# The two float32r parts of a unit of weights, interleaved column by column in one tile

## The chip, the cores and the metric

The kernel runs on one core of one Trainium2 chip. The metric is the device time of one execution, in microseconds (us). The kernel before was run twice: 1192.42 and 1192.73 us, median 1192.58 us. TensorE (PE in the rows) multiplies a stationary operand of up to 128 columns, which a weight load (PEld) puts into the array, with a moving operand of up to 512 columns; it writes to PSUM. VectorE (DVE), ScalarE (ACT) and GpSimd (POOL) work beside it, and SyncE (SP) issues most DMAs.

## The reference

A decoder trunk of two layers over 512 tokens with 1024 channels, all in float32. Layer 0 mixes tokens with an mLSTM (4 heads, projections for q, k, v, o and gates, output projection). Layer 1 mixes them with a convolution module (1024 to 2 x 1024 projection with a gate, depthwise convolution over 31 tokens, layer norm, output projection). After each mixer comes a gated MLP: a projection up to 2 x 2816 channels, a depthwise convolution over 3 tokens, `silu(a) * b`, a projection down to 1024. There is an RMS norm ahead of every mixer and MLP and one at the end:

```
x = x + mixer_i(rmsnorm(x, norm_mix[i]))
hdn = causal_dwconv(rmsnorm(x, norm_ffn[i]) @ w_up, conv_w, conv_b)
x = x + (silu(hdn[..., :D_FF]) * hdn[..., D_FF:]) @ w_down
```

## The kernel before

Activations lie with channels on partitions and tokens along the free axis: `xt[m]` is a block of 128 channels by 512 tokens. TensorE takes float32r operands, and full precision comes from splitting each operand into two float32r parts, a rounded copy (hi) and the rest (lo). A product of two float32 blocks is then three products, hi x hi, hi x lo and lo x hi, which `mm3` issues one after the other (L161 to L163); each has its own weight load.

**Weights** come in 193 units of at most 128 x 1024 float32, in the order of the list `seq`. `feed_to` issues the DMA of a unit on SyncE's queue (tile `wr`, four buffers, up to four units ahead of the one in use). It then splits the unit two units ahead (in two places one): ScalarE writes the hi part with a copy (L149) and VectorE the lo part with a subtraction (L150). The two parts are two tiles, `wh` and `wl`, from the pool `wsp` with three buffers each, and each is contiguous: column c of a part is 4 bytes after column c - 1. `next_unit` hands the pair to the stage that uses it.

**Who reads the parts.** Units 0 to 3 and 5 to 8 are the v weights; in `v_pair` they are the moving operand (512 columns at a time) and the activations are stationary. Unit 4 holds the gate weights, stationary in slices of 36 columns that start 144 bytes apart. In the 184 units from the ninth on (q, k, o, output projection, up and down projections, the convolution module's projections) slices of 128 columns of `wh` and `wl` are the stationary operand, and the activations move: `xh`/`xl` in `proj`, `gh`/`gl_` and `zh`/`zl` in `out_proj` (L576, L577, L580), `yh`/`yl` in the down projection of `ffn`. The last block of the last down projection runs in two halves of 256 tokens, so its three units are used with moving operands of 256 columns.

**What orders the work.** The program is written in one order, and a planner with its own cost estimates orders each engine's queue; semaphores between writers, readers and the release of buffers follow from the tiles. A buffer of `wsp` can be written again when the products that read it are done. In the convolution module VectorE also computes taps of the depthwise convolution (L744, `dve_tap`), handed out between the projections' products. A 128 x 128 constant, `p128`, is set by GpSimd at the start of that module, cast by ScalarE to `pdvr`, and used for one mean; it lies in the module's pool `cp`. The pool `work` has four buffers with the tag `tmp` for short-lived tiles.

Of the kernel before, what the change touches and what calls it, by code (L numbers as in the profile page):

```python
# [9 lines left out]
F32 = mybir.dt.float32  # L10
F32R = mybir.dt.float32r
# [3 lines left out]
P = 128  # L15
# [9 lines left out]
EPS = 1e-6  # L25
QSCALE = 128.0 ** -0.5
NEG = -1.0e30
NPH = 4                    # token phases of the convolution on the tensor engine
NTAU = T // NPH
NJ = (CK + 2 * NPH - 3) // NPH  # L30
GR = 68                    # rows: input gates at 0, running maximum at 32, forget gates at 64

# column offsets in the packed per-channel parameter array
_COLS = {}
_off = 0
for _n, _w in [("norm_mix", 16), ("norm_ffn", 16), ("norm_final", 8), ("mconv_w", 32),
# [9 lines left out]
def hybrid_trunk(ctx, tc, x_in, par_in, tph_in, wg_in, wv_in, wqk_in, wo_in, mout_in, cin_in,  # L46
# [6 lines left out]
    wsp = ctx.enter_context(tc.tile_pool(name="wsp", bufs=3))  # L53
    work = ctx.enter_context(tc.tile_pool(name="work", bufs=1))
# [12 lines left out]
    def small():  # L67
        return psms.tile([P, T], F32, tag="ms", name=nm("ms"))

# [1 line left out]
    par = const.tile([P, NPAR], F32, name="par")  # L71
    nc.scalar.dma_start(out=par[:, :16], in_=par_in[:, :16])

# [18 lines left out]
    G.memset(mhalf, -0.5)  # L92

    def warm(n, after=None):
        """Products that nobody reads, to keep the clock of the tensor engine up over a wait."""
        ps = bank()
        for _ in range(n):
            with tc.issue_after(after.ins) if after is not None else nullcontext():
                after = PE.matmul(ps[:, :P], ones, ones, start=True, stop=True)  # L99

# [1 line left out]
    seq = []  # L102
    for h in range(2):
        for u in range(4):
# [3 lines left out]
    for what in "q0 o0 o1 q1 o2 o3 q2 o4 q3 o5 o6 o7".split():  # L108
        i = int(what[1])
# [22 lines left out]
    st = {"dma": 0, "split": 0, "get": 0}  # L132
    raws, splits = {}, {}

    def feed_to(ndma, nsplit):
        while st["dma"] < min(ndma, len(seq)):
            i = st["dma"]
            ap, n = seq[i]
            r = wraw.tile([P, 1024], F32, tag="wr", name=f"wr{i}")
            nc.sync.dma_start(out=r[:, :n], in_=ap)  # L140
            raws[i] = r
            st["dma"] += 1
        while st["split"] < min(nsplit, len(seq)):
            i = st["split"]
            n = seq[i][1]
            r = raws.pop(i)
            hi = wsp.tile([P, 1024], F32R, tag="wh", name=f"wh{i}")
            lo = wsp.tile([P, 1024], F32R, tag="wl", name=f"wl{i}")
            st["last"] = A.copy(hi[:, :n], r[:, :n])  # L149
            V.tensor_tensor(out=lo[:, :n], in0=r[:, :n], in1=hi[:, :n], op=ALU.subtract)  # L150
            splits[i] = (hi, lo)
            st["split"] += 1
# [9 lines left out]
        PE.matmul(ps, lh, rl, start=False, stop=False)  # L162
        PE.matmul(ps, ll, rh, start=False, stop=stop)  # L163

# [1 line left out]
    xh = [None] * KD  # L166
    xl = [None] * KD

# [27 lines left out]
        return t[:, c].rearrange("p (a b) -> p a b", b=P)  # L196

    def to_rows(src, c, tag):
        """Values along the free axis, equal on all partitions -> [128 tokens, blocks]."""
        nb = (c.stop - c.start) // P  # L200
        dg = work.tile([P, T], F32, tag="tmp", name=nm("dg"), bufs=4)
        V.tensor_tensor(out=blocks(dg, c), in0=src,
                        in1=ident[:].unsqueeze(1).to_broadcast([P, nb, P]), op=ALU.mult)
        r4 = work.tile([P, NTB], F32, tag=tag, name=nm(tag))
        V.tensor_reduce(out=r4[:, :nb], in_=blocks(dg, c), op=ALU.add, axis=mybir.AxisListType.X)
        return r4

    def from_rows(r4, nb, pb):
        """[128 tokens, blocks] -> the values along the free axis on all partitions (PSUM)."""
        hl = work.tile([P, 2, NTB], F32R, tag="hl", name=nm("hl"))  # L210
        V.tensor_copy(hl[:, 0, :nb], r4[:, :nb])
        V.tensor_tensor(out=hl[:, 1, :nb], in0=r4[:, :nb], in1=hl[:, 0, :nb], op=ALU.subtract)
        for i in range(2):
            dg = work.tile([P, NTB, P], F32R, tag="tmp", name=nm("dgr"), bufs=4)
            v = V.tensor_tensor(out=dg[:, :nb], in0=ident[:].unsqueeze(1).to_broadcast([P, nb, P]),
                            in1=hl[:, i, :nb].bitcast(F32).unsqueeze(2).to_broadcast([P, nb, P]),
                            op=ALU.mult)
            p = PE.matmul(pb, onesr, dg[:, :nb].rearrange("p a b -> p (a b)"), start=i == 0, stop=i == 1)  # L218
        return v, p

    def col_mean(ps, t, c, w):
        """Sum over the partitions of t times the constant in w, on all partitions."""
        h = work.tile([P, T], F32R, tag="tmp", name=nm("ch"), bufs=4)
        l = work.tile([P, T], F32R, tag="tmp", name=nm("cl"), bufs=4)
        A.copy(h[:, c], t[:, c])
        V.tensor_tensor(out=l[:, c], in0=t[:, c], in1=h[:, c], op=ALU.subtract)
        PE.matmul(ps, w, h[:, c], start=True, stop=False)
        PE.matmul(ps, w, l[:, c], start=False, stop=True)
# [4 lines left out]
        return o4  # L233

    def row_sums(ps, t, c, w, start, stop):
        """Adds the sums over the partitions of t, times w, to ps: [128 tokens, 2 * blocks]."""
        nb = (c.stop - c.start) // P
        for b in range(nb):
            s = slice(c.start + b * P, c.start + (b + 1) * P)
            PE.matmul(ps[:, 2 * b : 2 * b + 2], t[:, s], w[:, :2], start=start and b == 0,  # L240
                      stop=stop and b == nb - 1)

    def norm_rows(nrm, c):
        """1 / rms of the tokens in c, [128 tokens, blocks]."""
        n = c.stop - c.start
        ps = small()
        col_mean(ps[:, :n], nrm.acc, c, invdr)
        r4 = to_rows(ps[:, :n].rearrange("p (a b) -> p a b", b=P), c, "ms4")
        V.tensor_scalar(out=r4[:, : n // P], in0=r4[:, : n // P], scalar1=EPS, scalar2=None,
                        op0=ALU.add)  # L250
        return rsqrt4(r4, n // P, "rs4")

    # the row factors of a norm are worked out between the first products of the next stage
    hooks = []

    def run_hook():
# [15 lines left out]

    rs = {}

    # ================= layer 0: mLSTM =================
    warm(9)
    nrm = Norm()
    first = wraw.tile([P, 1024], F32, tag="wr", name="wr0")
    for c in range(2):
        cs = slice(c * T, c * T + T)  # L280
        nc.sync.dma_start(out=first[:, cs], in_=seq[0][0][:, cs])
        nc.sync.dma_start(out=xt[c], in_=x_in[c])
    hi = wsp.tile([P, 1024], F32R, tag="wh", name="wh0")
    lo = wsp.tile([P, 1024], F32R, tag="wl", name="wl0")
    for c in range(2):
        cs = slice(c * T, c * T + T)
        A.copy(hi[:, cs], first[:, cs])
# [67 lines left out]

    pv = v_pair(0)

    # gates, channel-major: input gates on partitions 0-3, forget gates on 32-35
    wgh, wgl = next_unit()
    pg = small()  # L360
    for k in range(KD):
# [77 lines left out]
    T0 = [0, 128, 256, 256]  # L439

    def att_decay(h):
        """exp of the decay from s to t less the running maximum; s on partitions, t free."""
        plf, pm = small(), small()
        for p, i in ((plf, h), (pm, NH + h)):
            PE.matmul(p, sel[:, i, :], sth, start=True, stop=False)
# [143 lines left out]
    out_proj(gh, gl_, None, lambda m: ("norm_ffn", m))  # L589
    mctx.close()  # L590

    # ================= gated MLP with a depthwise convolution =================
    def ffn(l, g=None, last=False):
        fctx = ExitStack()
        fp = fctx.enter_context(tc.tile_pool(name=nm("ffn"), bufs=1))
# [94 lines left out]

    ffn(0, lambda m: ("norm_mix", 8 + m))

    # ================= layer 1: convolution module =================
    cctx = ExitStack()
    cp = cctx.enter_context(tc.tile_pool(name="conv", bufs=1))
    DVE_CH, POOL_CH, PE_CH = (0, 2, 4), (1,), (3, 5, 6, 7)
    NV, NG, NG4, NPRE = 5, 4, 9, 1
    cacc2 = cp.tile([P, T], F32, name="caccp")
    p128 = cp.tile([P, P], F32, name="p128")
    G.memset(p128, 1.0 / P)  # L700
    pdvr = cp.tile([P, P], F32R, name="pdvr")
    A.copy(pdvr, p128)
    cacc = {c: cp.tile([P, T], F32, name=f"cacc{c}") for c in range(8)}
    # 1 where the partition lies in the block of NPH partitions
    tph = cp.tile([P, 8 * 4 * NJ * NPH], F32, name="tph")
    nc.sync.dma_start(out=tph, in_=tph_in)
    msk4 = cp.tile([P, P // NPH, 1], F32, name="msk4")
# [74 lines left out]
                o = 32 * (2 * hf + g)  # L782
                (nc.scalar if g == 0 else nc.sync).dma_start(out=back[o : o + 32], in_=co[:, g])

    # taps for the vector engine and GpSimd, handed out between the products
    vtaps, gtaps = [], []

    def background(nv, ng):
# [9 lines left out]
    FIRST, LAST = PE_CH[0], PE_CH[-1]  # L798

    def shift():  # L800
        """The mean of one block of channels, by which all values are shifted before their sums."""
        d[FIRST] = cp.tile([P, T], F32, name=f"d{FIRST}")
        A.activation(d[FIRST].rearrange("p (t q) -> p t q", q=NPH),
                     cacc[FIRST].rearrange("p (q t) -> p t q", q=NPH), AF.Identity,
# [56 lines left out]
    sq4 = stats(4, V)  # L861
    sq7 = stats(LAST, None)

    # layer norm over channels
    pr1, pr2, pmu = small(), small(), bank()
    for i, (t1, t2) in enumerate(((s1, s2), (d[LAST], sq7))):
        row_sums(pr1, t1, slice(0, T), invd, i == 0, i == 1)
# [34 lines left out]
def _layout(inputs):  # L902
    f = {k: np.asarray(v) for k, v in inputs.items()}

    def ch(a):  # [..., C] -> [128, ... * C/128], channel c = m * 128 + p
        a = a.reshape(a.shape[:-1] + (-1, P))
        return np.moveaxis(a, -1, 0).reshape(P, -1)

    def taps(w):  # [K, C] -> [128, C/128 * K]
        k, c = w.shape  # L910
        return w.reshape(k, c // P, P).transpose(2, 1, 0).reshape(P, -1)

    def cols(w, n=P):  # [K, N] -> [N/n, 128, K/128 * n]
        k, c = w.shape
        return w.reshape(k // P, P, c // n, n).transpose(2, 1, 0, 3).reshape(c // n, P, -1)

    # gate biases: input gates on partitions 0-3, forget gates on 32-35
    bg = np.zeros((P, 1), np.float32)
    bg[0:4, 0], bg[32:36, 0] = f["m_b_gates"][0][:4], f["m_b_gates"][0][4:]
    # taps by token phase: dph[c * NPH + p, m, g, j, q] = w[K - 1 - (NPH * j + q - p), m * 128 + g * 32 + c]  # L920
    dw = f["c_dw_w"][0].reshape(CK, KD, 4, P // 4)
    dph = np.zeros((P // NPH, NPH, KD, 4, NJ, NPH), np.float32)
    for p in range(NPH):
# [50 lines left out]
```

## Time and profile before

| | |
|---|---|
| median of two runs | 1192.58 us (1192.42 to 1192.73) |
| profiled execution, first to last instruction | 1191.0 us |
| runs' median over that span | 1.6 us |
| TensorE matmul busy | 1134.3 us, 95% |
| weight loads busy | 939.7 us, 79% |
| VectorE busy | 788.6 us, 66% |
| ScalarE busy | 510.8 us, 43% |
| mean granted TensorE clock | 0.974 |

The share of busy matmul time is an upper view, since matmuls overlap in the records: one of 512 columns is recorded with about 390 ns although the next starts some 230 ns after it. So the start-to-start time, called the pitch below, is read from the records in order of time, and not from their durations.

### The profile page before, as it was taken

To read this page: it belongs to the slowest core of one execution; us is meant where nothing else is said; L and a number is where in the kernel's file an instruction comes from. 1 tells how busy PE (TensorE), PEld (TensorE's weight loads), DVE (VectorE), ACT (ScalarE), POOL (GpSimd) and SP (SyncE) were. 2 spreads that over 40 slices of the span, in tenths; PEclk is the share of its full clock that TensorE was granted. 3 is DMA by queue.
4 is the path that set the end of the run, shared out by engine and by line. 5 is a ranking of instruction groups with operands and counts; after the bars stand their busy time and mean duration, and the time that the engine had idled before them with its cause. 6 is when DMAs were issued, how large, how long until landed. Compare 5 with 4: busy or idle time off the path is not lost.

```text
span 1191.0 us, 13476 instructions
## 1 busy us (share of the span) xinstructions
PE 1134.3 (95%) x5226; PEld 939.7 (79%) x5226; DVE 788.6 (66%) x1022; ACT 510.8 (43%) x713; POOL 174.8 (15%) x126
## 2 busy tenths in 40 slices
PE   9999999999999999999998757699999999999996
PEld 7788888888888888888887647588888888888886
DVE  6788875487777775332479999874877777752222
ACT  6556774354444443222244522363544444432221
POOL 4000001100000000000267857021000000000002
PEclk9999999999999999999998879699999999999998
DMA  6222123223232323233332112022232323233322
GB/s 247 89 89 71 54 74 103 90 89 106 89 106 89 105 86 92 90 97 98 110 105 62 62 44 67 14 88 89 92 103 90 106 89 106 84 98 89 93 62 71
DMA packets 36369, 106.85 MB, mean 90 GB/s; under 512 B 4049, under 2 KB 10321, under 8 KB 36305
## 3 DMA queue, kind: packets, MB, share of 16 engines
q1 hardware_dynamic: 31728, 103.25, 27.2%
q10 hardware_dynamic: 4576, 2.74, 0.8%
q8 instruction: 41, 0.67, 0.2%
q14 instruction: 24, 0.19, 0.0%
HBM read 101.78 MB, written 2.10 MB: 87 GB/s over the span
## 4 chain that ended last, share of the span: by engine, by line
PE 84%; DVE 13%; issue 1%; ACT 1%; DMA 1%; POOL 0%; ACTq 0%; POOLq 0%; SPq 0%; DVEq 0%
PE mm L161 25%; PE mm L162 25%; PE mm L163 25%; DVE cacc L744 8%; PE mm L580 2%; PE mm L577 2%; PE mm L576 2%; DVE wl L150 2%; PE ms L240 1%; PE mm L99 0%; DMA xall<-in_dram 0%; PE ms L218 0%; DVE u L722 0%; DVE se L453 0%; DVE s L826 0%
## 5 line engine op out<-in xcount | busy, mean ns | idle before, releaser
L163 PE MATMUL mm<-xh,wl 128*128 128x512 f32 x960 | 375.6, 391 | 3.3 <-DVE wl L150 3.3
L161 PE MATMUL mm<-xh,wh 128*128 128x512 f32 x960 | 375.6, 392 | 0.0
L162 PE MATMUL mm<-xl,wh 128*128 128x512 f32 x960 | 375.4, 391 | 0.0
L150 DVE TENSOR_TENSOR wl<-wr,wh 128x1024 fp32r<-128x1024 f32 (+1 forms) x192 | 236.5, 1235 | 165.5 <-ACT wh L149 163.3
L149 ACT CAST wh<-wr 128x1024 fp32r<-128x1024 f32 (+1 forms) x192 | 197.4, 1030 | 296.1 <-PE mm L162 243.6
L163 PEld LDWEIGHTS mm<-xh,wl 128*128 128x128 f32 x960 | 181.4, 189 | 41.9 <-DVE wl L150 3.7
L162 PEld LDWEIGHTS mm<-xl,wh 128*128 128x128 f32 x960 | 181.4, 189 | 37.9
L161 PEld LDWEIGHTS mm<-xh,wh 128*128 128x128 f32 x960 | 181.5, 189 | 37.2
L193 POOL TENSOR_TENSOR acc<-acc,sq 128x512 f32<-128x512 f32 x30 | 43.3, 1444 | 746.7 <-ACT sq L191 746.2
L161 PE MATMUL mm<-yh,wh 128*128 128x512 f32 (+1 forms) x374 | 142.3, 380 | 0.0
L162 PE MATMUL mm<-yl,wh 128*128 128x512 f32 (+1 forms) x374 | 142.3, 380 | 0.0
L163 PE MATMUL mm<-yh,wl 128*128 128x512 f32 (+1 forms) x374 | 142.2, 380 | 0.0
L606 DVE TENSOR_TENSOR mm<-mm,rsb 128x512 f32<-128x512 f32 x88 | 60.8, 695 | 76.0 <-PE mm L163 73.1
L744 DVE SCALAR_TENSOR_TENSOR cacc<-u,par,cacc 128x501 f32<-128x501 f32 (+27 forms) x80 | 102.1, 1321 | 0.1
L161 PEld LDWEIGHTS mm<-yh,wh 128*128 128x128 f32 x374 | 70.0, 187 | 15.5
L162 PEld LDWEIGHTS mm<-yl,wh 128*128 128x128 f32 x374 | 70.0, 187 | 15.3
L163 PEld LDWEIGHTS mm<-yh,wl 128*128 128x128 f32 x374 | 70.0, 187 | 15.2
L616 ACT CAST yh<-ta 128x512 fp32r<-128x512 f32 x44 | 27.3, 620 | 104.6 <-DVE ta L615 104.6
L611 DVE SCALAR_TENSOR_TENSOR ta<-mm,par,ta 128x511 f32<-128x511 f32 x88 | 65.6, 745 | 1.3
L611 DVE SCALAR_TENSOR_TENSOR tb<-mm,par,tb 128x511 f32<-128x511 f32 x88 | 65.5, 746 | 1.4
L614 ACT ACTIVATE ta<-ta 128x512 f32<-128x512 f32 x44 | 27.8, 632 | 79.4 <-DVE ta L611 79.4
L741 POOL TENSOR_TENSOR cacc<-cacc,cprod 128x511 f32<-128x511 f32 (+29 forms) x30 | 49.5, 1651 | 24.1 <-ACT cprod L739 22.4
(237 smaller groups left out, 1200.5 us busy)
## 6 DMA issues: line engine op xcount, KB each, us to landing
wr<-in_dram SPq DMA_DIRECT2D x175, 512.0 KB, 3.5
wr<-in_dram SPq DMA_DIRECT2D x16, 384.0 KB, 3.1
xall<-in_dram SPq DMA_DIRECT2D x8, 256.0 KB, 6.4
us<-u ACTq DMA_DIRECT2D x16, 64.0 KB, 2.1
out_dram<-xall SPq DMA_DIRECT2D x2, 384.0 KB, 3.5
tph<-in_dram SPq DMA_DIRECT2D x1, 576.0 KB, 4.5
wr<-in_dram SPq DMA_DIRECT2D x2, 256.0 KB, 3.9
cacc<-co ACTq DMA_DIRECT2D x8, 64.0 KB, 2.4
```

What stands on the lines that cost most here:

```text
L149: st["last"] = A.copy(hi[:, :n], r[:, :n])
L150: V.tensor_tensor(out=lo[:, :n], in0=r[:, :n], in1=hi[:, :n], op=ALU.subtract)
L161: PE.matmul(ps, lh, rh, start=start, stop=False)
L162: PE.matmul(ps, lh, rl, start=False, stop=False)
L163: PE.matmul(ps, ll, rh, start=False, stop=stop)
L193: e.tensor_tensor(out=nrm.acc[:, c], in0=nrm.acc[:, c], in1=sq[:, c], op=ALU.add)
L606: V.tensor_tensor(out=ps, in0=ps, in1=rs["b"], op=ALU.mult)
L611: V.scalar_tensor_tensor(out=t[:, s:], in0=ps[:, : T - s], scalar=pcol("fconv_w", m * 3 + 2 - s), in1=t[:, s:], op0=ALU.mult, op1=ALU.add)
L614: A.activation(ta, ta, AF.Silu)
L616: A.copy(yh[:, j, :], ta)
L741: G.tensor_tensor(out=a[:, s:], in0=a[:, s:], in1=p[:, s:], op=ALU.add)
L744: V.scalar_tensor_tensor(out=cacc[j][:, s:], in0=u[:, : T - s], scalar=dw(j, CK - 1 - s), in1=cacc[j][:, s:], op0=ALU.mult, op1=ALU.add)
```

## The change

The two parts of a unit become two views of one tile of 2112 columns, from one tag with three buffers. For units 0 to 8 the views are two contiguous halves. From unit 9 on the tile is read as pairs: hi is every even column and lo every odd one, so a part's columns lie 8 bytes apart, and the pair starts at 4 x (unit number mod 16) columns, which is a multiple of 16 bytes from 0 to 240. The instructions that write and read the parts are the same in kind, number and size; only their addresses and strides differ. The pool `wsp` grows by 3 x 64 columns, 768 bytes per partition, and what is allocated behind it moves by as much. `p128` moves from the module's pool to a `tmp` buffer. Comments are removed.

```
+    def split_tile(i):
+        t = wsp.tile([P, 2048 + 64], F32R, tag="wi", name=f"wi{i}")
+        if i < 9:
+            return t[:, :1024], t[:, 1024:2048]
+        o = 4 * (i % 16)
+        v = t[:, o : o + 2048].rearrange("p (c b) -> p b c", b=2)
+        return v[:, 0], v[:, 1]
...
-            hi = wsp.tile([P, 1024], F32R, tag="wh", name=f"wh{i}")
-            lo = wsp.tile([P, 1024], F32R, tag="wl", name=f"wl{i}")
+            hi, lo = split_tile(i)
             st["last"] = A.copy(hi[:, :n], r[:, :n])
             V.tensor_tensor(out=lo[:, :n], in0=r[:, :n], in1=hi[:, :n], op=ALU.subtract)
...
-    p128 = cp.tile([P, P], F32, name="p128")
+    p128 = work.tile([P, P], F32, tag="tmp", name="p128", bufs=4)
```

## Rows read from the trace of the kernel before

**Rows 1.** The page's busy times: engine, us, share of the span, instructions.
```profile
PE 1134.3 (95%) x5226; PEld 939.7 (79%) x5226; DVE 788.6 (66%) x1022; ACT 510.8 (43%) x713; POOL 174.8 (15%) x126
```

**Rows 2.** The page's chain that ended last, shares of the span by engine.
```profile
PE 84%; DVE 13%; issue 1%; ACT 1%; DMA 1%; POOL 0%; ACTq 0%; POOLq 0%; SPq 0%; DVEq 0%
```

**Rows 3.** Busy time by window: us, PE, PEld, DVE, ACT, POOL, clock, DMA.
```profile
300.00:400.00 100.00, 100.00 (x442) 82.78 (x442) 73.62 (x93) 43.50 (x55) 0.00 (x0) 1.00 0.31 99
500.00:550.00 50.00, 50.00 (x216) 40.09 (x215) 14.13 (x15) 13.57 (x16) 3.85 (x3) 1.00 0.33 97
600.00:757.00 157.00, 113.33 (x609) 97.31 (x607) 149.25 (x138) 58.85 (x86) 102.05 (x59) 0.87 0.21 64
1163.00:1180.00 17.00, 17.00 (x149) 16.91 (x147) 3.34 (x9) 3.50 (x6) 2.18 (x3) 1.00 0.00 1
```

**Rows 4.** Groups by line and form on PE: count, busy us, mean ns, idle before.
```profile
L161 PE MATMUL mm<-xh,wh 128*128 128x512 f32 x960 | 375.6, 392 | 0.0
...
L161 PE MATMUL mm<-yh,wh 128*128 128x512 f32 x330 | 130.0, 394 | 0.0
...
L576 PE MATMUL mm<-gh,wh 128*128 128x512 f32 x48 | 18.9, 394 | 0.0
...
L161 PE MATMUL mm<-yh,wh 128*128 128x256 f32 x44 | 12.3, 279 | 0.0
```

**Rows 5.** PE in order of time, an up projection: start us, duration us, instruction.
```profile
300.28 0.39 PE L161 MATMUL mm<-xh,wh 128*128 128x512 f32 x1
...
306.40 0.39 PE L161 MATMUL mm<-xh,wh 128*128 128x512 f32 x1
```

**Rows 6.** PE in order of time, the last down projection with 512 columns.
```profile
1156.67 0.39 PE L162 MATMUL mm<-yl,wh 128*128 128x512 f32 x1
...
1163.20 0.39 PE L163 MATMUL mm<-yh,wl 128*128 128x512 f32 x1
```

**Rows 7.** PE in order of time, the last block, 256 columns.
```profile
1163.43 0.28 PE L161 MATMUL mm<-yh,wh 128*128 128x256 f32 x1
...
1172.17 0.28 PE L163 MATMUL mm<-yh,wl 128*128 128x256 f32 x1
```

**Rows 8.** PE in order of time, the output projection of layer 0.
```profile
188.32 0.39 PE L576 MATMUL mm<-gh,wh 128*128 128x512 f32 x1
...
193.89 0.40 PE L576 MATMUL mm<-gh,wh 128*128 128x512 f32 x1
```

**Rows 9.** PE in order of time, the gates: 36 stationary columns, 512 moving.
```profile
34.80 0.39 PE L161 MATMUL ms<-xh,wh 128*36 128x512 f32 x1
...
40.36 0.40 PE L163 MATMUL ms<-xh,wl 128*36 128x512 f32 x1
```

**Rows 10.** Groups by line and form of the weight loads.
```profile
L161 PEld LDWEIGHTS mm<-xh,wh 128*128 128x128 f32 x960 | 181.5, 189 | 37.2
...
L161 PEld LDWEIGHTS ms<-xh,wh 128*36 128x36 f32 x8 | 0.9, 111 | 0.8
```

**Rows 11.** Groups by line and form on DVE: the split; a strided and a plain write.
```profile
L150 DVE TENSOR_TENSOR wl<-wr,wh 128x1024 fp32r<-128x1024 f32 x14 | 21.7, 1548 | 3.0 <-ACT wh L149 2.9
...
L722 DVE SCALAR_TENSOR_TENSOR u<-mm,par,sg 128x512 f32<-128x512 f32 x4 | 4.5, 1129 | 0.0
...
L727 DVE SCALAR_TENSOR_TENSOR u<-mm,par,sg 128x512 f32<-128x512 f32 x4 | 2.9, 740 | 0.0
```

**Rows 12.** Groups by line and form on ACT: split; strided read; plain.
```profile
L149 ACT CAST wh<-wr 128x1024 fp32r<-128x1024 f32 x175 | 183.6, 1052 | 250.5 <-PE mm L162 198.0 <-issue 38.8 <-PE mm L163 11.4
...
L803 ACT ACTIVATE d<-cacc,par 128x512 f32<-128x512 f32 x1 | 1.2, 1189 | 1.2 <-DMA cacc<-co 1.2
...
L735 ACT ACTIVATE cacc<-u,par 128x512 f32<-128x512 f32 x4 | 3.1, 808 | 0.0
```

**Rows 13.** Who waited for whom: us in total, times, longest us.
```profile
ACT wh L149 <- PE mm L162: 243.6, 137, 6.2
...
PE mm L163 <- DVE wl L150: 3.3, 1, 3.3
```

More of the change, by code (lines that the diff above doesn't have):

```diff
@@ L282, in hybrid_trunk @@
         nc.sync.dma_start(out=xt[c], in_=x_in[c])
-    hi = wsp.tile([P, 1024], F32R, tag="wh", name="wh0")
-    lo = wsp.tile([P, 1024], F32R, tag="wl", name="wl0")
+    hi, lo = split_tile(0)
     for c in range(2):
```

## The prediction

> **What bounds the kernel now.** I read the busy times first, then the chain that ended last, then the windows, and last the matmuls in order of time. TensorE is busy 95% of the span, and the chain runs through it for 84% and through VectorE for 13% [rows 1, 2]. The windows say where: in an up projection (300 to 400 us) and a down projection (500 to 550) TensorE has no idle time, while VectorE is busy 73.6 of 100 us and 14.1 of 50; in the convolution module (600 to 757) it is the other way round, VectorE 149 of 157 us and TensorE 113 [rows 3]. So outside the convolution module the time is the number of products times their pitch, the time from one start to the next.
>
> The pitch is what the reader should take from the rows, at a granted clock of 1.00 throughout (2.4 GHz). In the up projection 27 steps take 6.12 us, 226.7 ns each [rows 5]; in the down projection 28 steps take 6.53 us, 233.2 ns [rows 6]; in the output projection of layer 0, 24 steps take 5.57 us, 232.1 ns [rows 8]; with 256 columns, 77 steps take 8.74 us, 113.5 ns [rows 7]. 512 columns at 2.4 GHz are 213.3 ns and 256 are 106.7, so about 13, 20, 19 and 7 ns of each step are something else. Stages with the same columns and the same loads differ by 6.5 ns, and what they differ in is which tiles are read. Every 1 ns of pitch is worth 4.25 us: the products with strided weights are 3 x 960 with `xh`, 3 x 330 with `yh`, and 2 x 192 in the two output projections, of which the 48 of L576 in layer 0 are shown [rows 4], 4254 in all, and 3 x 44 with 256 columns.
>
> **The change, part by part.** Nothing is added or removed in number; five things move.
>
> *The weight loads read 128 columns 8 bytes apart instead of 4.* No load in the trace is strided, so the price is bounded. A load of 128 columns is recorded with 189 ns, one of 36 with 111 [rows 10]: 78 ns for 92 columns, 0.85 ns each, so about 109 ns of columns and 80 ns of something fixed. With 256 columns a load is done in every 113.5 ns [rows 7], so the fixed part is overlapped and a load takes no more than that of the path. At a pitch of 226.7 ns it could become twice as long before it sets the pitch. Lower end: nothing. Upper end: twice as long, 2 x 109 = 218 ns, which with the 13 ns that a 512-column step has over its columns makes 231 ns (if those 13 ns come on top; none if they don't). I take nothing. The moving operand is the nearest row for the rate: 512 columns of 4 bytes in 226.7 ns are 9.0 bytes per ns in each partition, and a load that sweeps 1024 bytes in 109 ns needs 9.4, about what a read here already does.
>
> *The start of each slice relative to the moving tile changes from unit to unit.* The gates are the nearest row: there the same moving tiles `xh`, `xl` meet slices that start 144 bytes apart, and 24 steps take 5.56 us, 231.7 ns [rows 9], although their loads are the shortest of all. So a short load does not give a short pitch, and something in the addresses or in the 36 columns costs 5 ns against [rows 5]. Lower end, if the offsets give every stage the pitch of the up projection: 990 x 6.5 + 192 x 5.4 ns (layer 0's output projection; I leave layer 1's as it is) = -7.5 us. Upper end, if they take it from the up and `proj` products: 2880 x 5.0 = +14.4 us, or 2880 x 6.5 = +18.7 us with the pitch of [rows 6]. Within one unit all slices keep one phase, so some units should stay where they are; I take +2 us.
>
> [...]
>
> *VectorE writes the lo part with a stride.* The nearest strided write is L722, 512 bytes from element to element: 1129 ns for 512 against 740 ns for the plain form L727 [rows 11], 0.76 ns per element more. For a split of 1024 columns that would be +0.78 us, the upper end; the lower end is nothing. In the up projection VectorE would rise from 73.6 to 73.6 + 18 x 0.78 = 88 of 100 us (18 splits to 100 us, since a unit's 24 steps take 5.44 us), still hidden. Where the cover is gone, in the convolution module, 14 splits lie in VectorE's way [rows 11], 10.9 us at the upper end. I take 0, because 8 bytes are nearer to 4 than to 512. ScalarE's copy has the same bounds: the one strided read there, L803, takes 1189 ns against 808 for L735 [rows 12], 0.74 ns per element, so at most +0.76 us a unit; ScalarE is busy 43.5 of 100 us in the up projection and waits for TensorE before most copies [rows 3, 13], so both ends are hidden and cost 0.
>
> [...]
>
> *One tile has one release.* If the halves of a tile are not told apart, the hi copy of a later unit waits for the last product of the old one instead of the last but one (0.23 us), or in the output projections for eight products more (8 x 232 ns = 1.9 us), and the first product of a unit waits for the lo part, two products earlier than now (0.45 us). ScalarE waits 137 times for that release [rows 13], but as a buffer's ordinary turn: a unit is split two units, 10.9 us, ahead, so the 1.9 us are hidden; behind the waiting copy stand ScalarE's activations for the next block, which have the unit's slack too. TensorE waited for the lo part once, 3.3 us [rows 13]; that wait starts 0.45 us earlier and ends when it did. With the cover gone the price is 0.45 us for each of some 14 units in the convolution module, where the products are not the bound. I take +0.5 us.
>
> *`p128` in a `tmp` buffer:* a memset on GpSimd and a cast of 128 columns once, each under the 0.8 us of the 512 columns of L735 [rows 12]; GpSimd has room there, a `tmp` buffer must be free first and returns after the cast. No SyncE or GpSimd DMA moves. Taken: 0; upper end 1 us.
>
> **Sum.** 0 + 2 + 0 + 0 + 0.5 + 0 = +2.5 us on the profiled execution, whose span is 1191.0 us; the runs' median is 1192.6, 1.6 us above it, so 1195 us.
>
> **The rivals.**
>
> *The phase is lost everywhere in `proj` (1209 us).* The offsets bring all 2880 products to 231.7 to 233.2 ns: +14.4 to +18.7 us, mean 16.5. For it: [rows 9]. Against: those rows have 36 columns as well. Within 2%.
>
> *Strided writes stop VectorE in the convolution module (1204 us).* +10.9 us as above. Within 2%.
>
> *The loads become the bound (1248 us), the other side of the forecast.* Place: every step. If a strided load takes twice as long and its fixed overlap does not hide, a 256-column step goes from 113.5 to about 227 ns, 132 x 113.5 = +15 us, and a 512-column step to twice the load plus the 20 ns of the down projection, 238 ns: 2880 x 11.3 + 990 x 4.8 + 384 x 6 = 32.5 + 4.8 + 2.3 = +40 us; 1192.6 + 55 = 1248. It decides from a load of some 1.95 times on, where 213 ns meet the columns. For it: loads and matmuls alternate one to one and no row shows a stride. Against: the rate above. Shorter of that, the 256-column steps alone give 1208 us.
>
> *The interleave frees the moving reads (1156 us).* If part of the 13 to 20 ns is the load's reads meeting the moving reads, and a load that sweeps at the same rate as the moving operand meets them less, the excess may fall to the 7 ns of [rows 7], a pitch of 220: 2880 x 6.7 + 990 x 13.2 + 384 x 12 = 19.3 + 13.1 + 4.6 = -37 us. For it: the excess depends on tiles. Against: the gates' short loads have no smaller excess.
>
> **How the numbers follow.** No visible change (1187 to 1200): 0.41. Phase lost: 0.22. Strided writes: 0.07. Loads bound: 0.17, of which 0.07 lies between 1217 and 1232. Freed reads: 0.13, of which 0.03 lies above 1165. The forecast is the likeliest, 1195 us. The range holds the first three and what is nearest of the others, 1165 to 1232 us; 0.1 is left out on each side. Its own case alone would be 1187 to 1200. A measurement of this kernel can tell about 2%, 24 us, from no change: faster 0.13, same 0.70, slower 0.17.
>
> **What would show it.** In the profile after: weight loads with `wi` at 189 ns and the pitch in the up and down projections at 226.7 and 233.2 ns would bear out the first two steps; loads near 300 ns, or 256-column steps above 115 ns, would show the bound rival; a pitch of 220 the freed reads. L150 at its old mean would clear VectorE, at 0.78 us more convict it. A granted clock below 1.00 in the projections, or VectorE at the head of TensorE's waits there, would make the sum wrong in a way that none of these cases has.

## The result, and the profile after

The changed kernel takes 1208.97 us (median of two runs, 1208.11 to 1209.84) against 1192.58 us: the ratio is 1.0137, 95% interval [1.0108, 1.0167]. It is slower, by less than the 2% that the chances were split at and by far more than the runs scatter. The time lies in the predicted range (1165 to 1232 us), but not in the case that the forecast was made for (1187 to 1200 us, 1195 us): it is that of the rival "the phase is lost everywhere in `proj`" (1209 us).

The page after: the span and the busy times, which have the shape of [rows 1].

```profile
span 1206.4 us, 13466 instructions
...
PE 1147.5 (95%) x5226; PEld 969.6 (80%) x5226; DVE 784.8 (65%) x1022; ACT 516.6 (43%) x713; POOL 181.7 (15%) x126
```

The windows that answer to [rows 3], an up projection, a down projection and the convolution module: TensorE is still without idle time in the first two at a granted clock of 1.00, but starts 433 products in 100 us where it started 442.

```profile
300.00:400.00 100.00, 100.00 (x433) 83.89 (x432) 70.40 (x91) 43.54 (x54) 0.00 (x0) 1.00 0.30 95
500.00:550.00 50.00, 50.00 (x217) 41.95 (x216) 16.61 (x18) 14.86 (x18) 5.66 (x4) 1.00 0.34 96
600.00:757.00 157.00, 121.53 (x647) 105.35 (x645) 145.90 (x131) 60.28 (x84) 110.12 (x61) 0.89 0.22 66
```

TensorE in order of time after (start, duration): first the first and last product of 40 units of the up projection, 959 steps apart, where [rows 5] had 226.7 ns a step; then the block with 256 columns, 76 steps.

```profile
246.82 0.40 PE L170 MATMUL mm<-xh,wi 128*128 128x512 f32 x1
...
469.63 0.39 PE L172 MATMUL mm<-xh,wi 128*128 128x512 f32 x1
...
1178.03 0.28 PE L170 MATMUL mm<-yh,wi 128*128 128x256 f32 x1
...
1187.17 0.28 PE L171 MATMUL mm<-yl,wi 128*128 128x256 f32 x1
```

That is 222.81 us / 959 = 232.3 ns, and 9.14 us / 76 = 120.3 ns against 113.5 [rows 7]. Summing the time from each product's start to the next one's, by the tile that moves, over both traces:

| moving tile, columns | products | before, us | after, us | mean step without waits, before to after |
|---|---|---|---|---|
| xh, xl (512) | 2880 | 685.9 | 701.2 | 226.8 to 232.3 ns |
| yh, yl (512) | 990 | 231.0 | 230.1 | 233.3 to 232.4 ns |
| zht, zlt (512) | 192 | 44.2 | 44.9 | 229.2 to 231.8 ns |
| gh, gl (512) | 192 | 44.9 | 44.7 | 232.4 to 232.0 ns |
| yh, yl (256) | 132 | 15.3 | 16.1 | 114.2 to 120.3 ns |
| all products | 5226 | 1182.6 | 1198.0 | |

(The last column leaves out the steps that contain a wait and those at a granted clock of 0.50.) The steps of all products, waits included, make up the span but for its two ends, so both grew by 15.4 us; what the table adds is where: 15.3 of it lies at the products with `xh` and `xl`. By stage, the two up projections took 11.7 us more; none of their 2112 steps holds a wait, and 2112 x 5.5 ns is 11.6. The q and o projections of layer 0 took 3.1 us more, 384 x 5.5 ns = 2.1 by the pitch and the rest in waits. The convolution module's projections took 0.5 us more instead of 2.1: their seven steps with a wait or a change of the clock grew from 28.7 to 29.9 us, but 8 whole steps instead of 21 lay in stretches with a granted clock of 0.50, where one takes 426.7 ns, and that is some 2.6 us less.

Such a stretch of the kernel before, its window and 13 products in order of time, the first and the last:

```profile
649.20:654.30 5.10, 5.10 (x13) 3.96 (x12) 5.10 (x5) 0.81 (x3) 3.66 (x3) 0.50 0.36 103
...
649.26 0.63 PE L161 MATMUL mm<-xh,wh 128*128 128x512 f32 x1
...
654.38 0.42 PE L161 MATMUL mm<-xh,wh 128*128 128x512 f32 x1
```

5.12 us / 12 = 426.7 ns at a clock of 0.50. Half of it, 213.3 ns, is the estimate for 512 columns at a clock of 1.00, 2.4 columns a ns.

The groups that answer to [rows 10, 11, 12], and the waits of [rows 13]:

```profile
L170 PEld LDWEIGHTS mm<-xh,wi 128*128 128x128 f32 x960 | 187.7, 196 | 36.1 <-DVE se L477 0.6
...
L159 DVE TENSOR_TENSOR wi<-wr,wi 128x1024 fp32r<-128x1024 f32 x175 | 222.6, 1273 | 182.3 <-ACT wi L158 182.1
L158 ACT CAST wi<-wr 128x1024 fp32r<-128x1024 f32 x175 | 196.4, 1125 | 283.0 <-PE mm L172 222.1 <-issue 58.9 <-ACT gt L379 1.0
...
PE mm L172 <- DVE wi L159: 1.6, 2, 1.2
```

The line of all 175 splits of 1024 columns on VectorE before, which [rows 11] show for the convolution module alone:

```profile
L150 DVE TENSOR_TENSOR wl<-wr,wh 128x1024 fp32r<-128x1024 f32 x175 | 220.7, 1264 | 165.5 <-ACT wh L149 163.3
```

A load went from 189 to 196 ns, ScalarE's split from 1052 to 1125, VectorE's from 1264 to 1273. ScalarE waits for L172 now, the last product of the old unit, and not for L162; TensorE's own wait for the lo part did not grow. So the loss is, but for some 1 us in the q and o projections and as much in the convolution module, not a wait and not a busy engine: in the stages with `xh` the step from one product to the next is 5.5 ns longer.

### The profile page after: what moved, and what is told of

Same layout as the page of the kernel before. It is cut to its first block, busy times and chain, and to the rows that moved or that the text cites. A ratio compares the mean times of both kernels' runs of the same rounds, so it can differ in the third digit from the quotient of the medians.

```text
span 1206.4 us, 13466 instructions
## 1 busy us (share of the span) xinstructions
PE 1147.5 (95%) x5226; PEld 969.6 (80%) x5226; DVE 784.8 (65%) x1022; ACT 516.6 (43%) x713; POOL 181.7 (15%) x126
## 4 chain that ended last, share of the span: by engine, by line
PE 82%; DVE 13%; issue 2%; ACT 1%; DMA 1%; POOL 0%; ACTq 0%; POOLq 0%; SPq 0%; DVEq 0%
PE mm L170 25%; PE mm L171 25%; PE mm L172 25%; DVE cacc L752 7%; PE mm L588 2%; PE mm L584 2%; PE mm L585 2%; DVE wi L159 2%; PE ms L249 1%; DVE se L461 1%; PE mm L99 0%; DVE u L730 0%; DMA xall<-in_dram 0%; DVE s L834 0%; DMA us<-u 0%
## 5 line engine op out<-in xcount | busy, mean ns | idle before, releaser
L172 PE MATMUL mm<-xh,wi 128*128 128x512 f32 x960 | 378.8, 395 | 1.6 <-DVE wi L159 1.6
L170 PE MATMUL mm<-xh,wi 128*128 128x512 f32 x960 | 379.2, 395 | 0.3 <-DVE se L477 0.3
L171 PE MATMUL mm<-xl,wi 128*128 128x512 f32 x960 | 378.7, 395 | 0.0
L159 DVE TENSOR_TENSOR wi<-wr,wi 128x1024 fp32r<-128x1024 f32 (+1 forms) x192 | 238.4, 1243 | 186.1 <-ACT wi L158 186.0
L158 ACT CAST wi<-wr 128x1024 fp32r<-128x1024 f32 (+1 forms) x192 | 211.1, 1102 | 327.4 <-PE mm L172 266.5
L172 PEld LDWEIGHTS mm<-xh,wi 128*128 128x128 f32 x960 | 187.6, 195 | 38.6 <-DVE wi L159 2.5
L170 PEld LDWEIGHTS mm<-xh,wi 128*128 128x128 f32 x960 | 187.7, 196 | 36.1 <-DVE se L477 0.6
L171 PEld LDWEIGHTS mm<-xl,wi 128*128 128x128 f32 x960 | 187.5, 195 | 35.6
L170 PE MATMUL mm<-yh,wi 128*128 128x512 f32 (+1 forms) x374 | 142.7, 382 | 0.0
L171 PE MATMUL mm<-yl,wi 128*128 128x512 f32 (+1 forms) x374 | 142.7, 381 | 0.0
L172 PE MATMUL mm<-yh,wi 128*128 128x512 f32 (+1 forms) x374 | 142.6, 381 | 0.0
L172 PEld LDWEIGHTS mm<-yh,wi 128*128 128x128 f32 x374 | 72.9, 195 | 12.4
L170 PEld LDWEIGHTS mm<-yh,wi 128*128 128x128 f32 x374 | 72.9, 195 | 12.4
L171 PEld LDWEIGHTS mm<-yl,wi 128*128 128x128 f32 x374 | 72.9, 195 | 12.4
```

The lines of the kernel that those rows point to most:

```text
L170: PE.matmul(ps, lh, rh, start=start, stop=False)
```

## The experiments

The first four runs part the change into its pieces. Theory 1: the pitch is set by the start address of the stationary slice against that of the moving tile. Theory 2: by the 8-byte stride. Theory 3: by the common tile and its waits. Addresses below are those that the program assigns: tiles `wh`, `wl`, `wi`, `xh` and `xl` start 64 bytes past a multiple of 256, `yh` and `yl` at a multiple, `zht` and `zlt` 128 past one. Slices of 128 columns are 512 bytes apart (1024 with the stride), so within a unit they all keep one difference.

**e1_no_rotation**, the stride alone.

```
-        o = 4 * (i % 16)
-        v = t[:, o : o + 2048].rearrange("p (c b) -> p b c", b=2)
+        v = t[:, :2048].rearrange("p (c b) -> p b c", b=2)
```

> The changed kernel with the pair of parts always at column 0 of its tile: the parts are still 8 bytes apart, only the rotation is gone. Theory 1 (the start address of the stationary slice against the moving tile sets the pitch): the phase is constant again as before the change, so the products with xh and xl go back to 226.8 ns and those with yh to 233.3; about 1193 us. Theory 2 (the 8-byte stride of the weight load sets the pitch, whatever its start): 232.3 ns stays; about 1208 us. Theory 3 (waits from the common tile): about 1208 us with the pitch at 226.8 and idle time instead.

Measured: 1211.83 us, ratio 1.0155 [1.014, 1.0171]. The products in order of time, an up projection, 27 steps:

```profile
346.69 0.39 PE L170 MATMUL mm<-xl,wi 128*128 128x512 f32 x1
...
352.99 0.39 PE L170 MATMUL mm<-xl,wi 128*128 128x512 f32 x1
```

6.30 us / 27 = 233.3 ns, and the same in every unit. The constant start did not bring 226.8 ns back: theory 1 as it stood is wrong, and theory 2's number is off too (233.3, not 232.3). The stride by itself costs 6.5 ns a step, and the rotation takes a little of that back.

**e2_no_stride**, the rotation alone.

```
-        if i < 9:
-            return t[:, :1024], t[:, 1024:2048]
-        o = 4 * (i % 16)
-        v = t[:, o : o + 2048].rearrange("p (c b) -> p b c", b=2)
-        return v[:, 0], v[:, 1]
+        o = 0 if i < 9 else 4 * (i % 16)
+        return t[:, o : o + 1024], t[:, o + 1024 : o + 2048]
```

> The changed kernel with contiguous parts one behind the other in the tile, the start rotating from unit to unit by 16 bytes as in the change: the rotation alone. Theory 1 (start address): xh products at 232 ns as in the changed kernel, about 1207 us. Theory 2 (stride): 226.8 ns and about 1192 us, loads back at 189 ns from 195. Theory 3 (common tile): about 1208 us.

Measured: 1206.29 us, ratio 1.0111 [1.0095, 1.0128], against theory 2's 1192. Two units of one stage in order of time, the first starting at column 0, the second at column 8 (32 bytes); first and last product of each, 23 steps:

```profile
396.30 0.39 PE L167 MATMUL mm<-xh,wi 128*128 128x512 f32 x1
...
401.51 0.39 PE L169 MATMUL mm<-xh,wi 128*128 128x512 f32 x1
...
407.19 0.39 PE L167 MATMUL mm<-xh,wi 128*128 128x512 f32 x1
...
412.55 0.39 PE L169 MATMUL mm<-xh,wi 128*128 128x512 f32 x1
```

5.21 / 23 = 226.5 and 5.36 / 23 = 233.0 ns (starts are shown to 0.01 us, so each is good to about 0.5 ns). Loads are back at 189 ns, so the rotation costs without making a load longer. Against the kernel before, the stride alone costs 19.0 us (e1), the rotation alone 13.5 and both together 16.4, so the two do not add up. This run also gives the whole curve: the mean step of the units, by their start (unit number mod 16).

| start, bytes | 0 | 16 | 32 | 48 | 64 | 80 | 96 | 112 | 128 | 144 | 160 | 176 | 192 | 208 | 224 | 240 |
|---|---|---|---|---|---|---|---|---|---|---|---|---|---|---|---|---|
| e2, xh, ns | 226.9 | 228.6 | 233.0 | 233.2 | 233.1 | 231.9 | 233.8 | 233.2 | 233.3 | 233.3 | 233.1 | 229.9 | 229.6 | 232.8 | 233.3 | 227.7 |
| e2, yh, ns | 233.1 | 231.5 | 234.1 | 233.1 | 233.5 | 233.3 | 233.2 | 229.8 | 229.4 | 232.6 | 233.2 | 227.7 | 226.8 | 227.0 | 232.9 | 233.2 |
| after, xh, ns | 233.0 | 233.5 | 232.3 | 231.3 | 230.8 | 231.9 | 232.9 | 230.0 | 231.3 | 233.4 | 233.4 | 233.3 | 233.3 | 231.9 | 233.4 | 231.5 |
| after, yh, ns | 231.3 | 232.4 | 233.2 | 230.0 | 231.5 | 233.5 | 233.4 | 233.3 | 233.2 | 231.9 | 233.5 | 231.5 | 233.1 | 233.5 | 232.9 | 231.2 |

The row of `yh` is that of `xh` moved by four places, 64 bytes, in both kernels: the 226.9 that `xh` has at 0 stands at 192 for `yh` (226.8), the 229.6 at 192 stands at 128 (229.4), and with the stride the 230.0 at 112 stands at 48. One place of the 32 is off by 1.6 ns (228.6 at 16 against 227.0 at 208), the others by 0.6 at most. 64 bytes is how far `yh` lies from `xh` modulo 256. So theory 1 has a new form: the pitch is a function of the stride and of the difference between the two addresses modulo 256 bytes. Contiguous slices have 226.7 ns near a difference of 0 and mostly 233 elsewhere; slices with the stride never have 226.7.

**e3_one_tile**, neither.

```
-        if i < 9:
...
-        return v[:, 0], v[:, 1]
+        return t[:, :1024], t[:, 1024:2048]
```

> The changed kernel with contiguous parts at column 0 for all units: neither stride nor rotation, only the common tile, the moved p128 and the 768 bytes more. Theories 1 and 2: pitches as before the change (226.8, 233.3), 1192 to 1194 us. Theory 3 (common tile): 1205 us or more.

Measured: 1194.18 us, ratio 1.001 [1.0001, 1.002], steps of 226.8 (`xh`) and 233.3 ns (`yh`). Theory 3 falls: common tile, release, `p128` and the shift of 768 bytes cost 1.4 us together. Nearly all of it is in layer 0's q and o projections, where the steps with a wait hold 1.2 us above the pitch before the change and 2.5 us here (2.4 in the changed kernel).

**e4_phase_of_down**, contiguous, the down projections' units moved under `yh`.

```
+        o = 48 if down[i] else 0
+        return t[:, o : o + 1024], t[:, o + 1024 : o + 2048]
```

> As e3_one_tile, but the units of the down projections start 192 bytes later, which gives their slices the same address modulo 256 bytes as the tiles yh and yl that move over them; all other units start at column 0 and have the address of xh and xl modulo 256. Theory 1 (start address against the moving tile): the yh products fall from 233.3 to 226.7 ns, 990 x 6.6 = 6.6 us less than e3_one_tile, 1186 us. Theory 2 (stride alone): no difference from e3_one_tile.

Measured: 1188.32 us, ratio 0.9963 [0.995, 0.9976]. A down projection in e3_one_tile and then in e4_phase_of_down, 27 steps each:

```profile
509.84 0.39 PE L167 MATMUL mm<-yl,wi 128*128 128x512 f32 x1
...
516.14 0.39 PE L167 MATMUL mm<-yl,wi 128*128 128x512 f32 x1
```

```profile
509.82 0.39 PE L171 MATMUL mm<-yh,wi 128*128 128x512 f32 x1
...
515.94 0.39 PE L171 MATMUL mm<-yh,wi 128*128 128x512 f32 x1
```

233.3 and 226.7 ns, as the theory said; 990 steps give 6.6 us, and the kernel is 5.9 us faster than e3_one_tile. What takes some back is the block with 256 columns: 114.2 ns a step at the old difference, 119.6 at 0, +0.7 us, which the expectation had not.

**e5_stride_best_offset**, the stride with one start per stage. `sh[i]` is 12 columns for the down projections, 44 for the convolution module's output projection and 28 elsewhere.

```
-        o = 4 * (i % 16)
+        o = sh[i]
```

> The changed kernel, parts 8 bytes apart, but with one fixed start per stage instead of the rotation, chosen so that every stage's slices start 112 bytes behind its moving tile modulo 256 bytes (28 columns for the xh stages, 12 for yh, 44 for zht). In the changed kernel the units with that difference had the lowest pitch, 230.0 ns. Theory 1, new form (the pitch is a function of stride and of the difference of the two addresses modulo 256 bytes): 230.0 ns for xh and yh products, so 2880 x 3.2 - 990 x 3.3 = +5.9 us on the 1194 us of e3_one_tile, 1199 to 1201 us. Rival (those units were low by chance of the stage they lie in): 232 to 233 ns, 1208 us.

Measured: 1200.16 us, ratio 1.0063 [1.0049, 1.0076]; 27 steps of an up projection:

```profile
346.67 0.39 PE L172 MATMUL mm<-xh,wi 128*128 128x512 f32 x1
...
352.88 0.39 PE L172 MATMUL mm<-xh,wi 128*128 128x512 f32 x1
```

6.21 / 27 = 230.0 ns, and 230.0 with `yh`. The curve holds where it is used as a plan, and the rival (chance of the stage) falls. The lowest of the 16 starts still loses against contiguous parts.

**e6_pads_before**, the kernel before, with the moving tiles shifted instead of the weights.

```
+        fp.tile([P, 16], F32, name=nm("pad"))
         yh = fp.tile([P, NF, T], F32R, name=nm("yh"))
...
+    cp.tile([P, 48], F32, name="pad")
     kb = cp.tile([P, T], F32, name="kb")
```

> The kernel before the change, two contiguous tiles per unit, with two unused pads of 64 and 192 bytes that move the moving tiles yh, yl and zht, zlt to the address of the weights modulo 256 bytes; no weight tile moves. Theory 1, new form: yh products 226.7 ns instead of 233.3 (-6.6 us), zht products 226.7 instead of 229.2 (-0.5 us), the 256-column products 119.6 instead of 114.2 (+0.7 us): 1186 us against 1192.6. Rival (the pitch hangs on the address of the weights alone): 1192.6 us.

Measured: 1187.57 us, ratio 0.9952 [0.9939, 0.9964]. 27 steps of a down projection:

```profile
509.69 0.39 PE L163 MATMUL mm<-yh,wl 128*128 128x512 f32 x1
...
515.81 0.39 PE L163 MATMUL mm<-yh,wl 128*128 128x512 f32 x1
```

226.7 ns again, with the weights where they were: it is the difference that counts, not the weights' own address. `zht` went from 229.2 to 227.2, the 256-column steps from 114.2 to 119.8. The gain is 5.2 us of the 6.4 that were expected. Two unused pads beat the kernel before by 0.5%, and the changed kernel by 1.8%.

**e7_rotate_256_bytes**, the period.

```
+        o = 0 if i < 9 else 64 * (i % 2)
+        return t[:, o : o + 1024], t[:, o + 1024 : o + 2048]
```

> As e2_no_stride (contiguous parts in one tile), but the start alternates between column 0 and column 64, 256 bytes, from unit to unit. Theory 1, new form, with a period of 256 bytes: 226.8 ns for xh products in all units and 233.3 for yh, 1194 us as e3_one_tile. Rival (any change of start from unit to unit costs, whatever its size, or a longer period): xh products above 230 ns in half of the units or all, 1199 us or more.

Measured: 1195.47 us, ratio 1.0018 [1.0009, 1.0027], and 226.8 (`xh`) and 233.3 ns (`yh`) in units of either start. In order of time, 44 steps over a unit that starts at column 0 and most of the next one, which starts at column 64:

```profile
349.99 0.39 PE L167 MATMUL mm<-xh,wi 128*128 128x512 f32 x1
...
359.96 0.39 PE L169 MATMUL mm<-xh,wi 128*128 128x512 f32 x1
```

9.97 us / 44 = 226.6 ns. Rotation as such costs nothing; a shift of 256 bytes can't be told from none, one of 128 can (233.3 in the table).

## Why the prediction was right or wrong

The forecast was 1195 us and the time 1209: inside the range, because the range was made to hold rivals as well, and not near the forecast. Two terms of the sum were too small, the loads' stride (taken at 0) and the start of the slices (taken at +2 us).

- **What bounds the kernel: right.** Outside the convolution module the time was products times pitch: the two up projections, 2112 products without a wait, took 11.7 us more, and 2112 x 5.5 ns is 11.6. The 213.3 ns that the forecast takes for 512 columns, at what it calls 2.4 GHz, are half of the 426.7 ns that the trace before shows at a clock of 0.50; 106.7 ns for 256 columns is half again.
- **The loads with a stride: wrong by the largest amount.** I took nothing, by the rate of the moving reads. The load itself is only 7 ns longer, 196 against 189, and a longer load does not go with a longer step: 230.0 ns with loads of 195 (e5), 233.0 with loads of 189 (e2). So the rival in which the loads become the bound (1248 us) is out, although one of its signs came, 256-column steps above 115 ns (120.3): e4 and e6 have 119.6 and 119.8 with contiguous loads of 188 ns, so that sign did not tell a load from an address. But the stride alone puts all `xh` products at 233.3 ns, +17.7 us in e1 against e3 (1211.8 - 1194.2). By 2880 x 6.5 it would be 18.7, the number that I had as the upper end of the next step and for another reason. The working asked only whether a load still fits under a product; what a strided load that fits does to the step was not a term. The stride cost VectorE's writes nothing, 1273 ns with it and 1274 without it in e3, but it did lengthen the loads and ScalarE's copy, 189 to 196 and 1052 to 1125 ns.
- **The start of the slices: the mechanism right, its size wrong, and it sank the forecast.** I took +2 us between -7.5 and +18.7 because "some units should stay where they are". With contiguous parts 1 start in 16 keeps 226.7 ns and its two neighbours part of it; with the stride none. The rotation alone is +12.1 us in e2 against e3 (1206.3 - 1194.2). For the rotation I should have taken the 231.7 ns that [rows 9] gave, which is also e2's mean over all `xh` products. That the row hit the size is in part luck, though. The gates' slices, 144 bytes apart, meet eight different differences, and the mean of e2's curve at those eight is 231.3 ns; but slice by slice they do not follow the curve. The slice at a difference of 0 has steps of 231.3 ns in the trace before and 232.3 in e2, where the curve has 226.9. So the 36 columns, which made me doubt the row, may well have a part in it; no run parts them from the offsets. The gain that I allowed in the down projection came out at -0.9 us, since 233.3 could only fall to the same mean.
- **The rival "the phase is lost everywhere in `proj`" (1209 us): the number hit, the cause half right.** It had the offsets take all 2880 products to 231.7 to 233.2 ns. They do stand at 232.3 and the kernel lost 16.4 us against its 16.5; but the rotation, its only cause, makes 12.1 of that by itself, and the stride, which it left out, makes 17.7 without any rotation. That the two together come out at its mean is luck.
- **That the offsets might change nothing** does not hold here: the difference of the two operands' addresses moves the pitch by 6.6 ns, from 233.3 in e3 to 226.7 in e4 and e6, at equal columns and loads of 187 and 188 ns.
- **VectorE's and ScalarE's writes: right.** VectorE's price was nothing, 1273 ns against 1274 in e3, and ScalarE's 73 ns a unit (1052 to 1125) lay under the products.
- **One tile, `p128`: right.** +0.5 us was taken, 1.4 us measured, with a ratio whose interval nearly reaches 1; the place was another, waits in layer 0's q and o projections and not in the convolution module.
- **The freed reads (1156 us): out.** No stage of any run has a mean step of 512 columns below 226.6 ns, with or without stride. What that rival rested on, that the excess depends on which tiles are read, was true (226.7 ns against 233.3 before the change); it did not follow that interleaving lowers it, and no run shows reads that meet, which it supposed.

What stays open is the mechanism inside: the runs give the step by the stride and by the difference of two addresses, and none shows what makes it so. A second low place, 229.6 to 229.9 ns at 176 to 192 bytes, has no explanation here. An interleave in groups of four columns, in which each group stays contiguous, was not tried, so whether the stride costs by its steps of 8 bytes or by the wider stretch that a load sweeps is open.

## What to carry to other kernels

Where TensorE is never idle, read the step between starts, stage by stage, to a tenth of a nanosecond: here stages with equal shapes had 226.7 and 233.3 ns, the addresses were the cause, and two pads of 64 and 192 bytes were worth 5.2 us (e6). Before a layout is made to rotate or interleave, look for a stage in the trace that already has such offsets (here the gates, whose mean came out right) and price the change with it. An access that fits in its time by its own rate may still lengthen the step: here loads of 193 to 196 ns fitted under steps of 226.7 ns, and the steps went to 233.3 (e1). So price what runs beside it as well.

## What the runs showed of the hardware

- With 128 x 128 float32r loads under 512 moving columns, contiguous, the step is 226.7 ns when both operands start at the same address modulo 256 bytes (e4, e6). Over 16 differences in steps of 16 bytes (e2, `xh`) it is 226.9 ns at 0, 227.7 to 229.9 ns at four others and 231.9 to 233.8 ns at eleven. A shift of 256 bytes changes nothing (e7, 226.8 ns at either start), one of 128 or 64 does (233.3 and 233.1 ns in e2).
- With stationary columns 8 bytes apart it is 230.0 to 233.5 ns at each of the 16 starts tried (the changed kernel; 233.3 in e1, 230.0 in e5).
- At a granted clock of 0.50 the step of 512 columns is 426.7 ns (before, 649 to 654 us).
- With 256 moving columns a difference of 0 is the worse of the two measured: 114.2 ns at 64 bytes (e3), 119.6 at 0 (e4).
- A load of 128 columns is recorded with 187 to 189 ns contiguous (before, e2, e3, e4, e6, e7) and 193 to 196 ns with a stride of 8 bytes (after, e1, e5). ScalarE's copy of 1024 columns takes 7% more with an output stride of 8 bytes (1125 ns after against 1052 before); VectorE's subtraction did not change (1273 ns after against 1274 in e3).
